# Splitting the modulation's first weights into two fp32r parts in a fused attention, mLSTM and expert block

## The chip, the cores and the metric

One core of one Trainium2 chip runs the whole program. The metric is the device time of one execution in microseconds (us). Five engines work side by side: TensorE (PE; its weight loads are listed as PEld), VectorE (DVE), ScalarE (ACT), GpSimd (POOL) and SyncE (SP), which here issues the DMAs.

## The reference, cut to what matters

One transformer block of depth 1 on 2048 tokens of width 1024, with 256 context tokens: modulation, an input projection, window attention and a two-way mLSTM beside each other, an output projection and an expert-choice FFN. The change is in the first two lines, of which `sh1` and `sc1` are needed before anything else can start:

```python
mod_x = silu(c)     @ w_mod + b_mod      # (1, 1024) @ (1024, 6144)
mod_c = silu(c_ctx) @ w_mod + b_mod
sh1, sc1, g1, sh2, sc2, g2 = split(mod_x, 6)          # the same split of mod_c
hx = rmsnorm(x, norm1_w) * (1 + sc1) + sh1            # 2048 tokens
hc = rmsnorm(ctx, norm1_w) * (1 + csc1) + csh1        # 256 context tokens
... = split(h @ w_in)                                 # 1024 x 2832, for hx and hc
```

## The kernel before, in words

The program has three phases: `phase_in` (modulation, projections, rope, convolution, window attention), `phase_mix` (mLSTM, output projection, router) and `phase_moe`. The change is in `phase_in`.

`phase_in` is written as coroutines (`Flow`). Each yields what it needs next: a token for a buffer (`tok[...]`), an event, or an engine with an estimated cost (`A(n)` ACT, `V(n)` DVE, `G(n)` POOL, `Q(n)` SP, or "P" with a number). A planner plays the engines through with these estimates and a priority for each coroutine (`PRI`, low number first), and emits the instructions in that order. So each engine has one fixed list and runs it strictly in order; a changed estimate or priority moves instructions far away from the edit. `BUFS` says how many buffers each name has.

- `mod_first` (L553) computes the two vectors' first 2048 columns of the modulation (shift and scale of the first norm). `sc8` holds silu(c) and silu(c_ctx): for each of the 8 blocks of 128 rows (k) and each of the 4 blocks of 512 columns (j) there are 8 stationary columns, of which two, at 2j and 2j+1, are not zero. So 32 matmuls (L593) in fp32 add up in one tile `rows` of 8x512. The weights come as `wm0` to `wm7`, 1 MB each, in `loads`. Then ACT copies `rows` out (L597), four small transposes (L603) turn it, and three DVE instructions (L608, L614) make `sh1` and `sc1`. In fp32 each of these matmuls is two records of the profile.
- `load_x` (L486) loads units of 256 tokens. `XW_AT` says behind which `wm` tile the first two units' loads (`xe`) and the first projection weights stand in SP's list. `norm_x` squares on ACT (L517), then scales on DVE (L522).
- `make_hx` (L628) transposes a unit (L689), applies scale and shift (`xv` or `hxv`, L653 and L658) and splits the result into `hx_hi` (rounded to fp32r) and `hx_lo` (the rest). `("x", 0)` is the first unit.
- `weights` (L702) loads the projection weights in pieces `w_raw` of 4 row blocks by 128 or 136 columns (three buffers), and `split_w` (L730) splits each into `w_hi` on ACT (L735) and `w_lo` on DVE (L741).
- `main` issues the projection as chains of 24 matmuls (L758, L776): hi by hi, lo by hi, hi by lo. The first group, "kv", goes unit by unit: x0, x1, then the context. Behind each kv chain stand rope and norm of the keys (`hxr`, `hr`, L947 to L966; products on POOL, L959 and L961), whose transposes (L1056 to L1058) stand in PE's list between later chains.

```python
rows = self.buf(self.ps, "o", [8, 512])
...
nc.tensor.matmul(rows, lhsT=sc8[:, k, j, :], rhs=ws[k][:, j * 512:(j + 1) * 512], ...)   # L593
```

## Time and profile before

| | |
|---|---|
| median of 3 runs | 2040.84 us (2037.56 to 2042.3) |
| the profiled execution | 2042.06 us |
| its span | 2040.3 us, so 1.8 us lie around it |
| TensorE busy | 91% of the span |
| VectorE, ScalarE, GpSimd busy | 78%, 63%, 41% |
| mean granted TensorE clock | 0.959 of full |

How to read it: times in rows are from the span's start. A busy TensorE is not a TensorE at its peak, since the ends of its matmuls are modelled and a later one starts while an earlier one drains; what one matmul costs in a run of them is the run's length by their number. A stall is worth what the chain of waits says it is worth in that stage, not the share of idle time over the whole span. The granted clock is 1.00 or 0.50 of full (2.4 or 1.2 GHz).

### The profile page before, as it was taken

To read this page: it belongs to the slowest core of one execution; us is meant where nothing else is said; L and a number is where in the kernel's file an instruction comes from. 1 tells how busy PE (TensorE), PEld (TensorE's weight loads), DVE (VectorE), ACT (ScalarE), POOL (GpSimd) and SP (SyncE) were. 2 spreads that over 40 slices of the span, in tenths; PEclk is the share of its full clock that TensorE was granted. 3 is DMA by queue.
4 is the path that set the end of the run, shared out by engine and by line. 5 is a ranking of instruction groups with operands and counts; after the bars stand their busy time and mean duration, and the time that the engine had idled before them with its cause. 6 is when DMAs were issued, how large, how long until landed. Compare 5 with 4: busy or idle time off the path is not lost.

```text
span 2040.3 us, 37000 instructions
## 1 busy us (share of the span) xinstructions
PE 1863.0 (91%) x12921; PEld 1665.6 (82%) x12921; DVE 1595.5 (78%) x3486; ACT 1280.7 (63%) x3144; POOL 839.1 (41%) x820
## 2 busy tenths in 40 slices
PE   7799999999999999996989989994589999999997
PEld 2698998899889989985767767783589999999996
DVE  3799779998998699868999677756667878787772
ACT  4477777787787777775665578865344545454542
POOL 0324234333543243316777665510334535353432
PEclk9899999999999999996999989996699999999999
DMA  8343264345342333227777867646467878888772
GB/s 281 98 145 102 73 189 123 109 149 160 99 120 79 95 84 97 79 82 205 270 255 260 286 224 242 225 145 222 133 203 210 261 226 253 240 235 254 223 233 42
DMA packets 293499, 357.82 MB, mean 175 GB/s; under 512 B 27288, under 2 KB 225592, under 8 KB 292416
## 3 DMA queue, kind: packets, MB, share of 16 engines
q1 hardware_dynamic: 283072, 320.32, 49.9%
q0 software_dynamic: 9376, 34.08, 7.2%
q8 instruction: 102, 1.67, 0.3%
q10 hardware_dynamic: 864, 1.05, 0.1%
q14 instruction: 85, 0.70, 0.1%
HBM read 270.73 MB, written 84.54 MB: 174 GB/s over the span
## 4 chain that ended last, share of the span: by engine, by line
PE 56%; DVE 24%; ACT 8%; DMA 6%; issue 5%; SPq 1%; POOL 0%; POOLq 0%; DVEq 0%; ACTq 0%
PE gu L2684 17%; PE mm L758 9%; PE yp L2736 8%; PE po L2004 5%; DVE w_lo L741 3%; PE t L303 2%; DMA w_raw<-in_w_in 2%; PE s L258 2%; PE o L593 1%; PE t L2628 1%; PE h L1912 1%; PE o L332 1%; PE o L331 1%; PE mm L776 1%; DVE s L280 1%
## 5 line engine op out<-in xcount | busy, mean ns | idle before, releaser
L2529 ACT ACTIVATE ew_hi<-ew_raw 128x1024 fp32r<-128x1024 f32 x184 | 193.6, 1056 | 163.6 <-PE yp L2736 91.5
L2457 DVE TENSOR_TENSOR ew_lo<-ew_raw,ew_hi 128x1024 fp32r<-128x1024 f32 x152 | 215.6, 1428 | 42.0 <-ACT ew_hi L2529 21.4
L291 POOL TENSOR_SCALAR P<-P,am 128x640 f32<-128x640 f32 (+1 forms) x128 | 113.1, 885 | 257.7 <-DVE am L289 145.4
L741 DVE TENSOR_TENSOR w_lo<-w_raw,w_hi 128x256 fp32r<-128x256 f32 (+1 forms) x352 | 157.3, 471 | 30.2 <-ACT w_hi L735 28.1
L2756 POOL DMA_INDIRECT out_x<-y,idx x32 | 57.1, 1786 | 260.7 <-DVE y L2750 175.0
L2684 PE MATMUL gu<-xg_hi,ew_hi 128*128 128x256 f32 x1024 | 148.6, 283 | 0.6 <-DVE xg_hi L2656 0.6
L758 PE MATMUL mm<-w_hi,hx_hi 128*128 128x256 f32 (+1 forms) x944 | 142.5, 288 | 5.2 <-ACT hxr L933 2.2
L735 ACT ACTIVATE w_hi<-w_raw 128x256 fp32r<-128x256 f32 (+1 forms) x352 | 135.2, 410 | 18.9 <-DMA w_raw<-in_w_in 18.1
L758 PE MATMUL mm<-w_hi,hx_lo 128*128 128x256 f32 (+1 forms) x944 | 141.9, 288 | 0.0
L2684 PE MATMUL gu<-xg_lo,ew_hi 128*128 128x256 f32 x1024 | 141.7, 280 | 0.0
L758 PE MATMUL mm<-w_lo,hx_hi 128*128 128x256 f32 (+1 forms) x944 | 141.5, 286 | 0.0
L2684 PE MATMUL gu<-xg_hi,ew_lo 128*128 128x256 f32 x1024 | 141.2, 280 | 0.0
L758 PEld LDWEIGHTS mm<-w_hi,hx_hi 128*128 128x128 f32 x944 | 124.8, 190 | 9.4 <-issue 2.7
L2684 PEld LDWEIGHTS gu<-xg_hi,ew_hi 128*128 128x128 f32 x1024 | 131.2, 189 | 1.0 <-DVE xg_hi L2656 0.9
L2684 PEld LDWEIGHTS gu<-xg_lo,ew_hi 128*128 128x128 f32 x1024 | 129.2, 189 | 0.0
L2684 PEld LDWEIGHTS gu<-xg_hi,ew_lo 128*128 128x128 f32 x1024 | 128.8, 189 | 0.0
L758 PEld LDWEIGHTS mm<-w_hi,hx_lo 128*128 128x128 f32 x944 | 125.0, 191 | 3.3 <-issue 2.6
L758 PEld LDWEIGHTS mm<-w_lo,hx_hi 128*128 128x128 f32 x944 | 124.6, 189 | 1.8 <-issue 0.9
L314 DVE TENSOR_TENSOR pl<-t,ph 128x512 fp32r<-128x512 f32 x156 | 105.8, 684 | 24.4 <-ACT ph L312 23.1
L282 ACT ACTIVATE P<-s,am 128x640 f32<-128x640 f32 (+1 forms) x128 | 99.8, 780 | 31.1 <-DVE am L280 25.7
L2750 DVE SCALAR_TENSOR_TENSOR y<-yp,gv,g2b 128x512 f32<-128x512 f32 x64 | 48.1, 751 | 90.2 <-PE yp L2736 90.2
L280 DVE CUSTOM_DVE_ANT_0 s<-s,mrow,nsink 128x640 f32<-128x640 f32 (+1 forms) x120 | 105.3, 877 | 13.1 <-PE s L262 7.5
(482 smaller groups left out, 5616.4 us busy)
## 6 DMA issues: line engine op xcount, KB each, us to landing
w_raw<-in_w_in SPq DMA_DIRECT2D x176, 256.0 KB
ew_raw<-in_w_gate SPq DMA_DIRECT2D x32, 1024.0 KB
ew_raw<-in_w_up SPq DMA_DIRECT2D x32, 1024.0 KB
ew_raw<-in_w_down SPq DMA_DIRECT2D x32, 1024.0 KB
xt<-in_w_mod SPq DMA_DIRECT2D x64, 256.0 KB
out_x<-xl SPq DMA_DIRECT2D x32, 512.0 KB
s_vs<-vsl SPq DMA_DIRECT2D x16, 516.0 KB
vsl<-s_vs SPq DMA_DIRECT2D x16, 516.0 KB
```

The source lines that it names most:

```text
L280: nc.vector.tensor_tensor_reduce(x, x, mask, 1.0, k.nsink[:, h:h + 1], op0=OP.add, op1=OP.min, accum_out=m[:, 0:1])
L282: nc.scalar.activation(P[:, :n], sc, AF.Exp, bias=m[:, 0:1], scale=-1.0, accum_out=m[:, 1:2])
L291: nc.gpsimd.tensor_scalar(P[:, :n], P[:, :n], m[:, 4:5], 0.0, op0=OP.mult, op1=OP.add)
L314: nc.vector.tensor_sub(lo, pt, f(hi))
L735: nc.scalar.activation(hi, raw[:, k:k + 2, :n], AF.Copy)
L741: nc.vector.tensor_sub(lo, raw[:, k:k + 2, :n], f(hi))
L758: self.nc.tensor.matmul(ps[:, :2 * n].rearrange("p (a b) -> p a b", a=2), lhsT=hx[:, k, t * 128:(t + 1) * 128], rhs=w[:, sl:sl + 2, k, :n] ...
L2004: self.nc.tensor.matmul(po, lhsT=m[:, k, :], rhs=self.wo[k0 + k][wi][:, sl], start=(j == 0), stop=(j == 11))
L2457: (self.nc.vector if eng == "D" else self.nc.gpsimd).tensor_sub(out, x, y)
L2529: nc.scalar.activation(hi[:, sl], raw[:, sl], AF.Copy)
L2684: nc.tensor.matmul(po[:, ft, :], lhsT=w[:, k, ft * 128:(ft + 1) * 128], rhs=x[:, k, :], start=(j == 0), stop=(j == 23))
L2736: nc.tensor.matmul(po[hf], lhsT=hs[i][h][:, ft, t * 128:(t + 1) * 128], rhs=wd[i][w][:, ft, hf * 512:(hf + 1) * 512], start=(j[hf] == 0), ...
```

## The change

The modulation's weights are split like the projection's: ACT rounds each 128x512 piece to fp32r (`mh`), and DVE takes the rest (`ml`), or POOL for the last piece of each of the first seven row blocks. silu is split as well (`sch` and the rest), and its two parts stand in 16 stationary columns instead of 8, hi at 2j and lo at 8+2j. Each piece then takes two fp32r matmuls against the same 16 columns, so that all four products add up in a tile of 16x512; two pieces of the last row block (`plain`) stay fp32. A ring of three buffers holds `mh` and `ml`. The four transposes become matmuls with `both` (two identities below each other), which add the two halves. The second unit's loads stand behind the first four pieces of projection weights (`w_first`) instead of before them, and the first unit's scaling and splitting (`hx0`) goes before everything else.

```diff
-XW_AT = (2, 6, 4, 7)
+XW_AT = (2, 7, 7, 7)
-PRI = dict(loadx=1, mod1=0, ..., hx0=1, ...)
+PRI = dict(loadx=1, mod1=0, ..., hx0=-1, ...)
-BUFS = dict(t=2, ...)
+BUFS = dict(mh=3, t=2, ...)
@@ load_x
                 if n < 2:
                     yield self.wm_ev[XW_AT[n]]
+                if n == 1:
+                    yield self.w_first
@@ mod_first
-        sc8 = p.tile([128, KT, 4, 8], F32, name="sc8")
-        nc.gpsimd.memset(sc8, 0.0)
+        s16, s16r = (p.tile([128, KT, 4, 16], dt, name=n) for n, dt in (("s16", F32), ("s16r", F32R)))
+        nc.gpsimd.memset(s16, 0.0)
+        sch = p.tile([128, KT, 2], F32R, name="sch")
+        both = p.tile([16, 8], F32, name="both")
...
-        for j in range(4):
-            yield V(16)
-            nc.vector.tensor_mul(sc8[:, :, j, 2 * j:2 * j + 2], self.c2, e)
-            fl.follow()
         yield V(16)
         nc.vector.tensor_mul(sc, self.c2, e)
+        yield V(16)
+        nc.vector.tensor_copy(sch, sc)
+        yield V(64)
+        nc.vector.tensor_copy(at(0), wide(f(sch)))
+        yield V(64)
+        nc.vector.tensor_sub(at(8), wide(sc), wide(f(sch)))
+        yield V2(512)
+        nc.vector.tensor_copy(s16r, s16)
+        yield V(8)
+        nc.vector.tensor_add(both, self.ident[0:16, 0:8], self.ident[0:16, 8:16])
...
+        plain = lambda k, j: k == KT - 1 and j < 2
...
-                if k == 0:
+                if k in (0, KT - 1):
...
+        def low(k, j, hi, lo, w):
+            if j == 3 and k < KT - 1:
+                yield G(512)
+                nc.gpsimd.tensor_sub(lo, w, f(hi))
+            else:
+                yield V(512)
+                nc.vector.tensor_sub(lo, w, f(hi))
...
+        def splits():
+            for k in range(KT):
+                for j in range(4):
+                    if plain(k, j):
+                        continue
+                    yield part[k][j]
+                    yield tok["mh"]
+                    hi, lo = (p.tile([128, 512], F32R, name=n, bufs=BUFS["mh"]) for n in ("mh", "ml"))
+                    w = ws[k][:, j * 512:(j + 1) * 512]
+                    yield A(512)
+                    nc.scalar.activation(hi, w, AF.Copy)
+                    fl.spawn(low(k, j, hi, lo, w), PRI["mod1"])
...
-                yield "P", 0.86
-                nc.tensor.matmul(rows, lhsT=sc8[:, k, j, :], rhs=ws[k][:, j * 512:(j + 1) * 512], ...)
+                if plain(k, j):
+                    yield part[k][j]
+                    yield "P", 0.86
+                    nc.tensor.matmul(rows, lhsT=s16[:, k, j, :], rhs=ws[k][:, j * 512:(j + 1) * 512], ...)
+                    continue
+                yield done[k][j]
+                yield "P", 0.46
+                for i, w in enumerate(pieces[k, j]):
+                    nc.tensor.matmul(rows, lhsT=s16r[:, k, j, :], rhs=w, ...)
+                fl.give(tok["mh"])
...
-            nc.tensor.transpose(pm[:, c, :], row8[:, c * 128:(c + 1) * 128], self.ident[:8, :8])
+            nc.tensor.matmul(pm[:, c, :], lhsT=row16[:, c * 128:(c + 1) * 128], rhs=both, start=True, stop=True)
@@ make_hx
-            fl.spawn(split(k2, pt, tag), PRI["hx0" if u == ("x", 0) else "hxsp"])
+            fl.spawn(split(k2, pt, tag), PRI["hx0"] + 0.1 * k2 if u == ("x", 0) else PRI["hxsp"])
@@ weights
+                    if n == 1:
+                        fl.fire(self.w_first)
```

SP's list between the loads of the first and of the second unit. The number in a name tells tiles apart; `xe` of before is the second unit here, `w_raw` are the projection weights. Before:

```order
L581 DMA wm_189<-in_w_mod 128x2048
L502 DMA xe_188<-in_x 128x1024
L502 DMA xe_199<-in_x 128x1024
L721 DMA w_raw<-in_w_in 128x4x128
L724 DMA w_raw<-in_w_in 128x4x8
```

With the change:

```order
L589 DMA wm_277<-in_w_mod 128x512 x4
L763 DMA w_raw<-in_w_in 128x4x128
L766 DMA w_raw<-in_w_in 128x4x8
L763 DMA w_raw<-in_w_in 128x4x128
L766 DMA w_raw<-in_w_in 128x4x8
L763 DMA w_raw<-in_w_in 128x4x128
L766 DMA w_raw<-in_w_in 128x4x8
L763 DMA w_raw<-in_w_in 128x4x128
L766 DMA w_raw<-in_w_in 128x4x8
L504 DMA xe_405<-in_x 128x1024
L504 DMA xe_413<-in_x 128x1024
```

The second unit has moved behind the fourth piece of weights, and that piece takes the first one's buffer.

ACT's list from the copy of the modulation's sums (`row`) to the first unit's `hx_hi`. Before, where the second unit's squares (L517 of `xe_188` and `xe_199`) stand ahead of the first of these rows:

```order
L597 ACTIVATE row_234<-o 8x512
L735 ACTIVATE w_hi<-w_raw 128x272 x2
L658 ACTIVATE xv_213<-t,sh_84,sc_83 128x256
L658 ACTIVATE xv_257<-tr,sh_84,sc_83 128x256
L735 ACTIVATE w_hi<-w_raw 128x272
L658 ACTIVATE xv_213<-t,sh_84,sc_83 128x256
L658 ACTIVATE xv_257<-tr,sh_84,sc_83 128x256
L735 ACTIVATE w_hi<-w_raw 128x272
L735 ACTIVATE w_hi<-w_raw 128x2x128
L663 ACTIVATE hx_hi_96<-xv_213 128x512
L735 ACTIVATE w_hi<-w_raw 128x2x128
L663 ACTIVATE hx_hi_96<-xv_257 128x512
```

With the change:

```order
L700 ACTIVATE xv_284<-t,sh_84,sc_83 128x256
L700 ACTIVATE xv_314<-tr,sh_84,sc_83 128x256
L700 ACTIVATE xv_284<-t,sh_84,sc_83 128x256
L700 ACTIVATE xv_314<-tr,sh_84,sc_83 128x256
L705 ACTIVATE hx_hi_96<-xv_284 128x512
L705 ACTIVATE hx_hi_96<-xv_314 128x512
L779 ACTIVATE w_hi<-w_raw 128x272
L519 ACTIVATE hxv,xss<-xe_405 128x1024
L519 ACTIVATE hxv,xss<-xe_413 128x1024
L779 ACTIVATE w_hi<-w_raw 128x2x128
L779 ACTIVATE w_hi<-w_raw 128x272
```

No weights stand between the first unit's scaling and its splitting any more; the second unit's squares stand behind both, and the eighth half piece of "kv" weights (the last row, 128x272) behind the squares.

PE's list at the context's kv chains (L758 before, L802 with the change; `hx_hi_386` and `hx_hi_588` are the context; the 128x128 rows of `hxr` are the ropes' transposes, one group of three for each 128 tokens). Before:

```order
L758 MATMUL mm<-w_hi,hx_hi_386 128x272 x4
L1056 MATMUL tr<-cst,hxr_428 128x128
L1057 MATMUL tr<-cst,gate 8x128
L1058 MATMUL tr<-cst,gate 8x128
L689 MATMUL tr<-cst,xt 128x128 x4
L1056 MATMUL tr<-cst,hxr_461 128x128
L1057 MATMUL tr<-cst,gate 8x128
L1058 MATMUL tr<-cst,gate 8x128
L758 MATMUL mm<-w_hi,hx_hi_386 128x272 x4
```

With the change:

```order
L1100 MATMUL tr<-cst,hxr_715 128x128
L1101 MATMUL tr<-cst,gate 8x128
L1102 MATMUL tr<-cst,gate 8x128
L802 MATMUL mm<-w_hi,hx_hi_588 128x272 x4
L1100 MATMUL tr<-cst,hxr_769 128x128
L1101 MATMUL tr<-cst,gate 8x128
L1102 MATMUL tr<-cst,gate 8x128
L731 MATMUL tr<-cst,xt 128x128 x8
L802 MATMUL mm<-w_hi,hx_hi_588 128x272 x4
```

All four rope groups (`hxr_715` and `hxr_769` are the third and fourth) now stand ahead of the context's second four matmuls; before, the third and fourth stood behind them.

## Rows read from the trace of the kernel before

**Rows 1.** Four stretches of the span: its bounds and length in us, busy us (and records) of each engine, then the granted clock, the share of the DMA engines and GB/s.

```profile
0.00:44.00 44.00, 33.53 (x92) 9.53 (x93) 11.63 (x46) 14.33 (x36) 0.65 (x6) 0.98 0.83 292
44.00:100.00 56.00, 43.59 (x301) 39.17 (x300) 41.58 (x130) 30.15 (x96) 14.78 (x22) 0.87 0.36 108
100.00:900.00 800.00, 768.62 (x5925) 723.88 (x5924) 699.51 (x1855) 607.86 (x1627) 286.82 (x408) 1.00 0.39 111
```

**Rows 2.** TensorE in order of time from the start: start us, length us, what, how many records, and in brackets the idle time before with what ended it.

```profile
7.79 25.88 PE L593 MATMUL o<-wm,sc 128*8 128x512 f32 x56 [7.79 <-DVE sc L561]
...
34.19 3.60 PE L593 MATMUL o<-wm,sc 128*8 128x512 f32 x8
...
39.18 0.41 PE L603 MATMUL mm<-cst,row 8*128 8x8 f32 x4
...
44.74 1.67 PE L758 MATMUL mm<-w_hi,hx_hi 128*128 128x272 f32 x8
...
52.01 1.17 PE L758 MATMUL mm<-w_lo,hx_hi 128*128 128x272 f32 x8
55.12 1.83 PE L758 MATMUL mm<-w_hi,hx_hi 128*128 128x272 f32 x8 [1.93 <-ACT hxr L933]
...
67.02 0.30 PE L1056 MATMUL tr<-cst,hxr 128*128 128x128 f32 x1 [0.52 <-issue]
...
73.67 1.09 PE L689 MATMUL tr<-cst,xt 128*128 128x128 f32 x4 [5.92 <-DVE gatet L1078]
75.97 0.45 PE L1056 MATMUL tr<-cst,hxr 128*128 128x128 f32 x1 [1.22 <-ACT hxv L658]
...
77.09 1.28 PE L758 MATMUL mm<-w_hi,hx_hi 128*128 128x272 f32 x4
```

**Rows 3.** DMA issues on SP and the first squares on ACT, in the same form.

```profile
17.70 0.38 SPq L721 DMA_DIRECT2D w_raw<-in_w_in  x1
...
35.32 0.37 SPq L721 DMA_DIRECT2D w_raw<-in_w_in  x1
...
17.71 1.06 ACT L517 ACTIVATE hxv<-xe 128x1024 bf16<-128x1024 f32 x1 [10.26 <-DMA xe<-in_x]
```

**Rows 4.** Windows of the modulation's stage, columns as in rows 1.

```profile
16.00:20.00 4.00, 4.00 (x11) 0.81 (x10) 0.00 (x0) 2.26 (x4) 0.00 (x0) 1.00 1.03 424
24.00:28.00 4.00, 4.00 (x11) 0.88 (x10) 0.00 (x0) 0.00 (x0) 0.00 (x0) 1.00 1.00 416
```

**Rows 5.** The nearest durations. First DVE at the preparation and at the first unit's scaling (first and last record), then DVE's and POOL's subtraction of 128x512 and ACT's rounding of 128x512, then a run of fp32r matmuls of 512 columns from the chain of waits (start us, length us).

```profile
7.56 0.43 DVE L561 TENSOR_TENSOR sc<-cols,sce 128x16 f32<-128x16 f32 x4 [0.36 <-ACT sce L551]
...
20.35 0.16 DVE L534 SCALAR_TENSOR_TENSOR rs_t<-xrs 128x1 f32<-128x1 f32 x1 [12.27 <-ACT xrs L532]
...
21.95 0.75 DVE L522 TENSOR_SCALAR xe<-xe,xrs 128x1024 f32<-128x1024 f32 x1
...
43.17 0.75 DVE L666 CAST hx_hi<-xv 128x512 fp32r<-128x512 f32 x2
...
47.04 1.29 DVE L670 TENSOR_TENSOR hx_lo<-xv,hx_hi 128x512 fp32r<-128x512 f32 x2
...
76.41 1.27 POOL L673 TENSOR_TENSOR hx_lo<-hxv,hx_hi 128x512 fp32r<-128x512 f32 x1 [2.20 <-DVE hx_hi L666]
...
43.18 0.63 ACT L663 ACTIVATE hx_hi<-xv 128x512 fp32r<-128x512 f32 x1
...
1528.50 10.90 PE yp L2736 x48
```

**Rows 6.** DVE and POOL at the same time, two places of the timeline.

```profile
251.56 2.19 DVE L741 TENSOR_TENSOR w_lo<-w_raw,w_hi 128x256 fp32r<-128x256 f32 x3
...
251.79 1.33 POOL L673 TENSOR_TENSOR hx_lo<-hxv,hx_hi 128x512 fp32r<-128x512 f32 x1 [2.43 <-PE mm L758]
...
1503.19 1.22 DVE L2457 TENSOR_TENSOR ew_lo<-ew_raw,ew_hi 128x1024 fp32r<-128x1024 f32 x1
...
1508.80 4.48 DVE L2457 TENSOR_TENSOR ew_lo<-ew_raw,ew_hi 128x1024 fp32r<-128x1024 f32 x1 [2.67 <-issue]
...
1508.56 1.29 POOL L2457 TENSOR_TENSOR xg_lo<-xv,xg_hi 128x512 fp32r<-128x512 f32 x1
1509.80 2.40 POOL L2457 TENSOR_TENSOR ew_lo<-ew_raw,ew_hi 128x1024 fp32r<-128x1024 f32 x1
```

**Rows 7.** Windows with TensorE partly idle, or just after idle time, columns as in rows 1.

```profile
8.00:10.00 2.00, 2.00 (x3) 0.27 (x2) 0.08 (x1) 0.00 (x0) 0.00 (x0) 1.00 1.05 436
12.00:14.00 2.00, 2.00 (x6) 0.45 (x5) 0.00 (x0) 0.00 (x0) 0.00 (x0) 1.00 1.00 422
42.00:44.00 2.00, 1.73 (x8) 1.73 (x9) 2.00 (x6) 1.81 (x5) 0.00 (x0) 0.50 0.92 250
62.00:66.00 4.00, 2.78 (x23) 2.32 (x21) 3.58 (x12) 2.92 (x10) 2.25 (x3) 1.00 0.00 0
1451.00:1457.00 6.00, 4.14 (x18) 3.37 (x19) 2.42 (x7) 3.07 (x7) 2.34 (x3) 0.50 0.04 3
```

**Rows 8.** What follows the modulation on ACT and DVE, in order of time: the copy of its sums, the first unit's first scaling, and the last product of the fourth rope.

```profile
37.83 0.59 ACT L597 ACTIVATE row<-o 8x512 f32<-8x512 f32 x1 [2.57 <-PE o L593]
...
40.42 0.57 ACT L658 ACTIVATE xv<-t,sh,sc 128x256 f32<-128x256 f32 x1 [1.37 <-DVE sc L614]
...
74.39 0.22 DVE L966 TENSOR_TENSOR hxr<-hxr,ropeu 128x64 f32<-128x64 f32 x1
```

More of the change, by code (lines that the diff above doesn't have):

```diff
@@ L456, in phase_in @@
             self.mod_ev, self.opened, self.main_done, self.rest_ev, self.turned = (Event() for _ in range(5))
-            self.att_ev, self.gt_ev = Event(), Event()
+            self.att_ev, self.gt_ev, self.w_first = Event(), Event(), Event()
             self.reach = {(b, g): Event() for b in range(4) for g in GROUPS}
@@ L581, in loads @@
                     nc.sync.dma_start(ws[k], a["w_mod"][k * 128:(k + 1) * 128, 0:2048])
+                    for ev in part[k]:
+                        fl.fire(ev)
                 fl.fire(self.wm_ev[k])
                 fl.issued()
+        def low(k, j, hi, lo, w):
[5 more added lines that the diff above has]
+                nc.vector.tensor_sub(lo, w, f(hi))
+            pieces[k, j] = hi, lo
+            fl.fire(done[k][j])
@@ L585, in mod_first @@
         fl.spawn(loads(), PRI["ml"])
+        fl.spawn(splits(), PRI["mod1"])
         for k in range(KT):
-            if k:
-                yield self.wm_ev[k]
             for j in range(4):
-                if not k:
-                    yield part[j]
-                yield "P", 0.86
-                nc.tensor.matmul(rows, lhsT=sc8[:, k, j, :], rhs=ws[k][:, j * 512:(j + 1) * 512],
-                                 start=(k == 0 and j == 0), stop=(k == KT - 1 and j == 3))
-        row8 = p.tile([8, 512], F32, name="row8")
+                if plain(k, j):
+                    yield part[k][j]
+                    yield "P", 0.86
+                    nc.tensor.matmul(rows, lhsT=s16[:, k, j, :], rhs=ws[k][:, j * 512:(j + 1) * 512], start=False, stop=False)
+                    continue
+                yield done[k][j]
+                yield "P", 0.46
+                for i, w in enumerate(pieces[k, j]):
+                    nc.tensor.matmul(rows, lhsT=s16r[:, k, j, :], rhs=w, start=(k + j + i == 0), stop=(k + j + i == KT + 3))
+                fl.give(tok["mh"])
@@ L596, in mod_first @@
+        row16 = p.tile([16, 512], F32, name="row16")
         yield A(512)
-        nc.scalar.activation(row8, rows, AF.Copy)
+        nc.scalar.activation(row16, rows, AF.Copy)
         fl.give(tok["o"])
@@ L609, in mod_first @@
                                  b.to_broadcast([128, 2, 2, 4]))
-            if j:
-                fl.follow()
+            fl.follow()
         fl.give(tok["mm"])
```

15 lines of the change are left out of this document (9 added, 6 removed).

## The prediction

> **What bounds the kernel now.** I read the chain of waits first, then the windows by stage, then the timelines of the first 100 us. From 100 to 900 us TensorE is busy 768.6 of 800 us at clock 1.00 [rows 1]: there a microsecond saved ahead of it is a microsecond saved at the end, and nothing that leaves TensorE's own work alone can bring much. The first 44 us have only 33.5 busy us of TensorE and the next 56 only 43.6 [rows 1]; the change works in these. The modulation's matmuls run without a pause from 7.79 to 37.79 us, with one group of transposes between them [rows 2]: TensorE is the bound there, not the DMA, which brings 416 to 424 GB/s throughout [rows 4]. The first projection chain starts at 44.74, the first unit's two chains end at 53.2, the second unit's first chain starts at 55.12, and from 67.4 to 77.1 TensorE has little but rope transposes to do; only at 77.09 does its continuous work begin [rows 2]. I call 37.79 the end of the modulation and 77.09 the point from which a shift is kept.
>
> **Term 1, the modulation's stage.** Removed: 64 fp32 records, 25.88/56 = 0.462 us each [rows 2], so 29.6 us of TensorE. Added: 60 fp32r matmuls at 10.90/48 = 0.227 us [rows 5] and 4 fp32 records, together 15.5 us. TensorE's need is halved, and the question is what becomes the bound.
> - DVE's preparation: six small instructions instead of five, of 0.2 us or less but for a cast of 512 columns (0.4); four of the five took 0.43 us [rows 5]. From 7.56 us I take 1.4 us, so the first subtraction can start at 9.0.
> - DVE subtracts 23 pieces (three in each of seven row blocks, two in the last). Two such instructions in a row took 1.29 and one takes 0.68, so 0.61 each [rows 5]: 14.0 us.
> - POOL subtracts 7 pieces of 1.27 us [rows 5]: 8.9 us. Do the two engines do it side by side? Rows of this case say no. At 251.56 three subtractions of 0.42 took 2.19 us, because one stood still while POOL's ran to 253.12; at 1508.80 one that takes 1.22 alone took 4.48, through two of POOL's, 1.29 and 2.40 [rows 6]. So one row block costs 3 x 0.61 + 1.27 = 3.1 us, above the 2.5 us in which 1.05 MB come at 420 GB/s [rows 4], and the sum is 22.9 us.
> - The first unit's scaling stays between the row blocks on DVE, 20.35 to 22.70 [rows 5]: 2.35 us. ACT's two squares, 1.06 us each [rows 3], now stand between roundings of 0.6 us [rows 5] for which DVE waits, and the second row block's data come a little late for DVE: 1.6 us together.
> - Tail: behind the last of POOL's pieces TensorE runs the two pieces left in fp32, 4 x 0.462 = 1.85, and two split ones, 0.9; 1.2 us of DVE's work in the sum runs beside that, so 1.6 more.
>
> 9.0 + 22.9 + 2.35 + 1.6 + 1.6 = 37.5, against 37.79: **-0.3 us**. Bounds: if POOL's subtractions fell into gaps of DVE and the DMA were the limit, 9.44 MB at 0.42 MB per us with 1.4 MB there at 8 us are in at 28, the last piece needs its rounding, subtraction and matmuls, and the stage ends near 31: -7. If TensorE ran at half clock, 60 x 0.454 + 4 x 0.92 = 30.9 from 9.0, and four groups of transposes make it 41.5: +3.7. I take the value by the exclusion, since two places of this trace show it.
>
> **Term 2, from there to the end of the first unit's kv chains.** The sums' copy starts at 37.83 and the first scaling at 40.42, 2.6 us later [rows 8], with transposes and weight splits between; with the change neither stands there, so 0.59 + 0.41 + three small DVE instructions give 1.6: -1.0. The first unit is then scaled and split without weights between, so `hx_hi` is there 4.7 us after the end of the modulation. But the eighth half piece of weights stands on ACT behind the second unit's two squares, which cost ACT nothing on the path before. They wait for a load that is issued only when the fourth piece of weights has its buffer: that issue stood at 35.32 [rows 3] and stays near 36.5, because the buffer is freed by DVE behind its last subtraction. I have the squares start at +5 us and the eighth half at +7.6, so the first chain's last two matmuls come at +8, against 46.41 - 37.79 = +8.6 before; then the second unit's normalization (two DVE instructions of 0.75 [rows 5]) holds up its transposes in the middle of the second chain. The two effects leave **-0.5 us**, bounds -2 (all of the shorter path stays) and +3 (second unit late by as much as its squares and scaling take, 2.1 + 1.5, less 0.6).
>
> **Term 3, to the continuous work.** The four rope groups now all stand ahead of the context's second four matmuls; before, two did. The fourth rope's last product was done at 74.39 [rows 8], before TensorE reached 77.09, so the two moved groups add no wait of their own unless the second unit comes later, and what TensorE has left afterwards is shorter by two groups of up to 1.1 us each (75.97 to 77.09 [rows 2]). **-1.0 us**, bounds -4 and +4 (one context tile's transposes, scaling and POOL subtractions earlier or later; POOL took 1.27 for each of four).
>
> **Term 4, the rest of the first phase.** The planner moves instructions everywhere up to 900 us and none behind. TensorE's idle time there is 31.4 us of 800 [rows 1]; I take 0 and keep +-3 for another order of the same work.
>
> **Sum.** -0.3 - 0.5 - 1.0 = -1.8 us, so the profiled execution's 2042.06 becomes 2040.3. The median of the runs shown, 2040.84, lies 1.2 us below the profiled execution, so I give **2039.0 us**. A measurement of this kernel can tell about 0.2% from no change, 4.1 us: faster is below 2036.8, slower above 2044.9.
>
> **Rivals.**
> - *Faster: the DMA becomes the bound.* POOL has only one piece in four and the ring of three lets ACT run ahead, so POOL's piece could start where DVE would wait anyway. Against it stand the two places of rows 6, for it that the second of them had two POOL instructions in a row and this stage never has. Term 1 is then -5 to -7, and with the others about -7.5: 2033. Chance 0.34.
> - *Slower: TensorE's clock.* Today TensorE starts slowly (3 records in 2 us from 8 us on, 6 at 12 us [rows 7]) and then works without a pause. With the change it has 8 x 0.227 = 1.8 us of work for each 3.1 us. From 62 to 66 us it was busy 2.78 of 4 us and kept 1.00, but from 1451 to 1457 it was busy 4.14 of 6 and stayed at 0.50, and behind the idle time before 42 us it was at 0.50 too [rows 7]. The price: +3.7 in term 1, and the first unit's chains entered at half clock, where eight 272-column matmuls took 1.83 us instead of 1.17 [rows 2], for some four groups of eight: +2.6; the other terms' gains are then -1.0. It decides if half clock holds for more than half of the stage, since below that the subtractions are the slower part. 2040.84 + 5.3 = 2046. Chance 0.16. The Trainium skill, "TensorE: Matmul & The Clock Gate", section "A second HAM failure mode: psum-queue depth-cycling", tells of a kernel whose TensorE paused briefly and often between groups of matmuls and swung between the two clocks. By that rule this stage would swing too and cost about half of the first price, 1.9 us; the trace has stretches for it and against it.
> - *Slower: the second unit comes late.* Its loads wait in SP's list behind a buffer that DVE frees only behind the modulation; if that moves squares, transposes and ropes back together, terms 2 and 3 are at their upper bounds, +7 - 0.3: 2047. For it: before, its loads stood ahead of all weights. Against it: ACT is busy with the first unit until they can be there. Chance 0.08.
>
> **How the numbers follow.** The forecast, no change that can be measured, has 0.42, and its own range, from half of each term's bounds, is 2036 to 2043. The first rival gives faster, 0.34, the other two slower, 0.24. The range reaches into the rivals' times: 2031.5 to 2046.5 leaves out the first rival's far end (all of -7 and a better order) and the ends of the two slow ones, 0.2 together.
>
> **What would show it.** Right: `mh` and `ml` in about 3.1 us for a row block, subtractions of DVE that take 1.9 us where one of POOL's begins in front of them, the copy of the sums near 37.5, and continuous work on TensorE from about 75 us. For the first rival: row blocks at 2.5 us and the copy near 31 to 33. For the second: clock 0.50 in most of 10 to 37 us and fp32r matmuls of 0.45. For the third: TensorE waiting for `xe` transposes beyond 54 us. The forecast is wrong if the copy comes by 33 or after 40, or if TensorE's idle time from 100 to 900 us changes by more than 3 us.

## The result: slower by 1.2%, and the profile after

The changed kernel took **2065.14 us** (median of 4 runs, 2063.97 to 2067.02) against 2041.57 of the kernel before on the same chip; ratio **1.0119, 95% interval 1.0102 to 1.0137**, some 24 us. The two profiled spans, 2040.3 and 2062.2 us, differ by 21.9. The forecast was 2039.0 with a range from 2031.5 to 2046.5: the change went the other way, and the time lies outside the range.

Windows of the changed kernel by stage, columns as in [rows 1], and then one window in the idle stretch:

```profile
0.00:44.00 44.00, 26.41 (x89) 9.18 (x89) 28.53 (x60) 27.17 (x56) 10.48 (x13) 0.91 0.79 273
44.00:100.00 56.00, 35.04 (x179) 29.18 (x180) 30.33 (x101) 26.43 (x82) 10.47 (x16) 0.64 0.20 58
100.00:900.00 800.00, 767.80 (x5896) 721.16 (x5895) 698.89 (x1849) 598.98 (x1605) 282.34 (x407) 1.00 0.40 115
...
74.00:94.00 20.00, 8.50 (x30) 4.52 (x30) 8.58 (x26) 6.55 (x22) 5.32 (x7) 0.50 0.06 16
```

Against [rows 1] the first 44 us have 7 busy us of TensorE less, as the split should bring. The next 56 have 179 records where 301 stood, at clock 0.64 and not 0.87. From 100 to 900 us the busy time hardly differs (767.8, 768.6). This points to the stretch between the modulation's end and 100 us; the milestones below show it. From 74 to 94 us TensorE is busy 8.5 of 20 us, and all of it at the lower level of 1.2 GHz.

TensorE of the changed kernel in order of time, the same places as [rows 2] (L731 is L689 of before, L802 is L758, L1100 to L1102 are L1056 to L1058, L1122 is L1078):

```profile
36.37 1.89 PE L631 MATMUL o<-wm,s 128*16 128x512 f32 x4
...
39.96 1.05 PE L646 MATMUL mm<-both,row 16*128 16x8 f32 x8 [0.68 <-ACT row L640]
43.97 1.73 PE L802 MATMUL mm<-w_hi,hx_hi 128*128 128x272 f32 x6 [2.96 <-ACT hx_hi L705]
47.50 0.82 PE L802 MATMUL mm<-w_hi,hx_hi 128*128 128x272 f32 x2 [1.80 <-ACT w_hi L779]
48.12 2.02 PE L802 MATMUL mm<-w_hi,hx_lo 128*128 128x272 f32 x8
...
59.90 1.27 PE L802 MATMUL mm<-w_hi,hx_hi 128*128 128x272 f32 x4 [2.15 <-DVE hx_hi L708]
63.88 0.82 PE L802 MATMUL mm<-w_hi,hx_hi 128*128 128x272 f32 x2 [2.70 <-DVE hx_hi L708]
...
72.78 0.63 PE L731 MATMUL tr<-cst,xt 128*128 128x128 f32 x4 [1.19 <-DVE gatet L1122]
74.76 0.45 PE L1100 MATMUL tr<-cst,hxr 128*128 128x128 f32 x1 [1.35 <-ACT hr L534]
75.00 0.42 PE L1101 MATMUL tr<-cst,gate 128*8 128x128 f32 x1
75.36 0.59 PE L1102 MATMUL tr<-cst,gate 128*8 128x128 f32 x2
79.46 1.08 PE L731 MATMUL tr<-cst,xt 128*128 128x128 f32 x4 [3.52 <-DVE gatet L1122]
81.71 0.45 PE L1100 MATMUL tr<-cst,hxr 128*128 128x128 f32 x1 [1.16 <-ACT hxv L700]
...
85.87 0.45 PE L1100 MATMUL tr<-cst,hxr 128*128 128x128 f32 x1 [1.77 <-DVE gatet L1122]
...
90.02 1.08 PE L731 MATMUL tr<-cst,xt 128*128 128x128 f32 x4 [2.97 <-DVE gatet L1122]
92.28 1.12 PE L731 MATMUL tr<-cst,xt 128*128 128x128 f32 x4 [1.17 <-ACT hxv L700]
...
95.03 0.82 PE L802 MATMUL mm<-w_hi,hx_hi 128*128 128x272 f32 x2 [1.18 <-DVE hx_hi L708]
```

Read the brackets from 72.78 to 92.28: each group of transposes waits for the copies of the group ahead of it, since all of them go through the one buffer `tr`. (The bracket at 74.76 names `hr`; ACT's last copy out of `tr`, `hxv`, ended at 74.67, 0.1 us before.) The continuous work, that is matmuls of the projection one behind the other, starts at 95.03, where it started at 77.09 [rows 2].

The kernel before had the first three of the context's four transposes ahead of the first rope (67.02 [rows 2]), between chains:

```profile
60.77 0.60 PE L689 MATMUL tr<-cst,xt 128*128 128x128 f32 x4
...
62.73 0.62 PE L689 MATMUL tr<-cst,xt 128*128 128x128 f32 x4
...
64.68 0.66 PE L689 MATMUL tr<-cst,xt 128*128 128x128 f32 x4 [0.82 <-ACT hxv L658]
```

Inside one of these turn-rounds, the rope that began at 81.71, on all engines (first and last of each kind): four ACT copies, four DVE subtractions and the gate's copy, then the next group may begin.

```profile
82.30 0.60 PE L1102 MATMUL tr<-cst,gate 128*8 128x128 f32 x2
...
82.93 0.27 ACT L1112 ACTIVATE kt<-tr 64x128 fp32r<-64x128 f32 x1 [1.32 <-PE tr L1102]
...
83.78 0.27 ACT L1114 ACTIVATE kt<-tr 64x128 fp32r<-64x128 f32 x1
84.08 0.28 DVE L1118 TENSOR_TENSOR kt<-tr,kt 64x128 fp32r<-64x128 f32 x1 [2.02 <-ACT kt L1114]
...
85.31 0.41 DVE L1122 COPY gatet<-tr 8x256 f32<-8x256 f32 x1
```

From the transpose at 81.71 to the next group's at 85.87 a rope holds `tr` for 4.16 us, of which TensorE works 1.2. A context transpose holds it for 2.25 (79.46 to 81.71). From 72.78 to 95.03 four context transposes hold it for 9.2 us and three ropes for 13.0: that is the whole 22.25 us (the last of them up to the matmul that needs its result). Before the change only one turn-round of a rope was waited for, 5.92 us [rows 2].

The milestones, in us from the span's start: the copy of the modulation's sums 37.83 before and 39.32 after, the first projection matmul 44.74 and 43.97, the end of the first unit's kv chains 53.2 and 57.5, of the second unit's 63.9 and 71.6, the continuous work 77.09 and 95.03, the first projection matmul of L776 (L820 after) 96.7 and 115.1, the last hi-by-hi one of L758 (L802) 906.1 and 927.2, the first of the experts 1456.6 and 1477.9. Eighteen of the 21 us are lost by 95 us.

What the 21 us consist of, from 40 us to that last hi-by-hi matmul (before, after):

```profile
40.00:906.00 866.00, 819.94 (x6278) 770.56 (x6278) 747.93 (x2003) 645.57 (x1742) 302.99 (x432) 0.99 0.39 111
```

```profile
40.00:927.00 887.00, 830.88 (x6285) 776.69 (x6286) 750.33 (x2010) 650.07 (x1751) 299.71 (x432) 0.97 0.38 109
```

TensorE's idle time grew from 46.1 to 56.1 us (length less busy), and its busy time by 10.9 us, at clock 0.97 in place of 0.99. So half of the loss is waiting and half is longer busy time. One us of the latter is the modulation's own transposes (39.96), which lay ahead of 40 us before. A part comes with the lower level of the clock. Its stretches up to 100 us, first of the kernel before, then of the changed one:

```profile
41.90:45.30 3.40, 3.03 (x14) 3.03 (x15) 3.40 (x10) 2.55 (x7) 0.00 (x0) 0.50 0.94 302
55.60:59.00 3.40, 3.40 (x17) 3.40 (x16) 2.73 (x11) 0.50 (x2) 0.00 (x0) 0.50 0.00 0
69.20:79.50 10.30, 4.61 (x18) 3.42 (x19) 5.75 (x23) 2.65 (x9) 3.81 (x7) 0.50 0.24 77
```

```profile
43.30:53.50 10.20, 7.72 (x32) 7.41 (x33) 8.49 (x25) 7.14 (x22) 0.00 (x0) 0.50 0.69 195
60.30:67.20 6.90, 4.20 (x18) 3.82 (x18) 6.06 (x24) 3.11 (x10) 1.41 (x3) 0.51 0.00 0
74.00:97.90 23.90, 11.37 (x43) 7.39 (x43) 9.01 (x27) 7.07 (x22) 6.63 (x8) 0.50 0.12 35
```

With one more such stretch of the kernel before behind 100 us (345.7 to 349.1) and two of the changed one (347.0 to 350.5, 418.7 to 422.1), TensorE was busy at the lower level for 14.5 us before and 30.2 after. Eight matmuls take 1.17 us at the upper level [rows 2] and 2.02 at the lower, so by an estimate these 15.7 us more cost 6.6 us. The remaining 3 us of longer busy time were not traced to a cause.

### The profile page after: what moved, and what is told of

It is laid out like the page before. It is cut to its first block, busy times and chain, and to the rows that moved or that the text cites. A ratio compares the mean times of both kernels' runs of the same rounds, so it can differ in the third digit from the quotient of the medians.

```text
span 2062.2 us, 37117 instructions
## 1 busy us (share of the span) xinstructions
PE 1867.1 (91%) x12925; PEld 1672.0 (81%) x12925; DVE 1616.3 (78%) x3510; ACT 1297.6 (63%) x3174; POOL 844.4 (41%) x827
## 4 chain that ended last, share of the span: by engine, by line
PE 55%; DVE 24%; ACT 8%; DMA 6%; issue 5%; POOL 1%; SPq 0%; POOLq 0%; DVEq 0%; ACTq 0%
PE gu L2728 17%; PE mm L802 9%; PE yp L2780 8%; PE po L2048 5%; DVE w_lo L785 3%; PE t L303 2%; DMA w_raw<-in_w_in 2%; PE s L258 2%; PE mm L820 2%; PE t L2672 1%; PE o L332 1%; PE o L331 1%; PE h L1956 1%; DMA wm<-in_w_mod 1%; DVE s L280 1%
## 5 line engine op out<-in xcount | busy, mean ns | idle before, releaser
L802 PE MATMUL mm<-w_hi,hx_hi 128*128 128x256 f32 (+1 forms) x944 | 146.1, 291 | 11.1 <-DVE hx_hi L708 6.0
L802 PE MATMUL mm<-w_lo,hx_hi 128*128 128x256 f32 (+1 forms) x944 | 141.9, 289 | 0.0
L802 PE MATMUL mm<-w_hi,hx_lo 128*128 128x256 f32 (+1 forms) x944 | 141.1, 289 | 0.0
L802 PEld LDWEIGHTS mm<-w_hi,hx_hi 128*128 128x128 f32 x944 | 126.9, 192 | 15.1 <-DVE hx_hi L708 7.0
L802 PEld LDWEIGHTS mm<-w_lo,hx_hi 128*128 128x128 f32 x944 | 126.1, 192 | 2.6 <-issue 1.7
L802 PEld LDWEIGHTS mm<-w_hi,hx_lo 128*128 128x128 f32 x944 | 125.7, 192 | 1.0 <-issue 0.4
```

Of the source, the lines that this page charges most:

```text
L802: self.nc.tensor.matmul(ps[:, :2 * n].rearrange("p (a b) -> p a b", a=2), lhsT=hx[:, k, t * 128:(t + 1) * 128], rhs=w[:, sl:sl + 2, k, :n] ...
```

## The experiments

Three theories were tested. Theory 1: the planner's new order puts the four ropes between the context's transposes, and the turn-round of `tr` is the loss. Theory 2: the split modulation itself comes late (half clock, late second unit). Theory 3: SP's list, blocked by the gate's stores, holds up loads.

The results together. "Ropes" is how many ropes stand ahead of the fourth context transpose on TensorE; then the start of the first matmul of L776 and of the last hi-by-hi one of L758 (whatever its line in that kernel), TensorE's idle and busy time from 40 us to there, and the time against the kernel before on the same chip. All columns but the last are of the one profiled execution, which for ctx_t and hx0_old took 5.7 and 4.8 us more than the median of the kernel, and for before_new_order 4.8 less.

| kernel | ropes | first L776 | last L758 | idle / busy | ratio (95%) |
|---|---|---|---|---|---|
| before | 1 | 96.7 | 906.1 | 46.1 / 819.9 | 1 |
| changed | 4 | 115.1 | 927.2 | 56.1 / 830.9 | 1.0119 (1.0102 to 1.0137) |
| split_only | 1 | 97.7 | 908.6 | 48.3 / 820.7 | 1.0005 (0.9995 to 1.0015) |
| order_only | 4 | 116.0 | 929.4 | 58.0 / 831.0 | 1.0110 (1.0084 to 1.0137) |
| ropes_last | 0 | 97.9 | 916.1 | 46.2 / 829.8 | 1.0053 (1.0036 to 1.0070) |
| ctx_t | 1 | 98.3 | 921.0 | 53.3 / 827.7 | 1.0075 (1.0058 to 1.0091) |
| hx0_old | 4 | 112.6 | 927.5 | 56.0 / 831.0 | 1.0116 (1.0099 to 1.0133) |
| xw_old | 2 | 100.5 | 911.5 | 48.1 / 822.9 | 1.0032 (1.0020 to 1.0045) |
| split_dve | 4 | 113.8 | 928.5 | 57.9 / 830.1 | 1.0117 (1.0099 to 1.0135) |
| before_ropes_last | 0 | 91.9 | 908.0 | 41.2 / 826.8 | 1.0008 (0.9998 to 1.0017) |
| before_new_order | 4 | 113.4 | 929.0 | 56.9 / 832.1 | 1.0137 (1.0118 to 1.0157) |
| after_old_order | 1 | 104.3 | 915.7 | 49.3 / 826.7 | 1.0034 (1.0022 to 1.0046) |
| dve_old_order | 1 | 100.0 | 910.0 | 47.6 / 822.4 | 1.0043 (1.0028 to 1.0058) |
| after_t | 4 | 111.3 | 927.7 | 56.5 / 831.5 | 1.0109 (1.0093 to 1.0125) |
| after_ropes_t | 4 | 107.9 | 925.7 | 54.9 / 831.1 | 1.0086 (1.0069 to 1.0103) |
| before_ropes_t | 1 | 92.3 | 905.7 | 44.1 / 821.9 | 0.9984 (0.9973 to 0.9995) |
| split_ropes_t | 1 | 92.0 | 905.1 | 42.3 / 822.7 | 0.9993 (0.9978 to 1.0008) |

**The two halves of the change.** split_only is the changed kernel with `XW_AT`, `w_first` and the priority `hx0` as before; order_only is the kernel before with those three as after.

```diff
 split_only
-XW_AT = (2, 7, 7, 7)
+XW_AT = (2, 6, 4, 7)
-                if n == 1:
-                    yield self.w_first
-hx0=-1 ... PRI["hx0"] + 0.1 * k2 if u == ("x", 0) else PRI["hxsp"]
+hx0=1 ... PRI["hx0" if u == ("x", 0) else "hxsp"]
```

> The split weights and the split vector alone, with the loads, the second unit's condition and the first unit's priority as before the change. Theory 1: the planner puts three context transposes ahead of the first rope, as before the change, so the loss goes: 2038 to 2046 us. Theory 2: the modulation is what is late, 2057 to 2066 us.

> The opposite half: the fp32 modulation of before, with the changed order of loads, the changed condition of the second unit and the changed priority. The planner puts all four ropes ahead of the context's second four matmuls here too. Theory 1: the loss is nearly whole, 2056 to 2066 us, with the continuous work starting at 90 to 96 us. Theory 2: 2037 to 2046 us, since the modulation is the one of before.

1.0005 and 1.0110, 2044.2 and 2064.1 us, both as theory 1 says. The split by itself moves the time by nothing that can be measured, the three lines of order bring nearly the whole loss. Theory 2 falls for the modulation; for the late second unit it is not decided yet, since `w_first` is among the three lines.

**Which line.** hx0_old gives back the priority alone, xw_old the loads alone.

```diff
 hx0_old
-hx0=-1 ... PRI["hx0"] + 0.1 * k2 if u == ("x", 0) else PRI["hxsp"]
+hx0=1 ... PRI["hx0" if u == ("x", 0) else "hxsp"]
 xw_old
-XW_AT = (2, 7, 7, 7)
+XW_AT = (2, 6, 4, 7)
-                if n == 1:
-                    yield self.w_first
```

> The changed kernel with the priority of the first unit's preparation as before; the changed order of the loads stays. In the planned order two ropes stand among x1's chains and two, not three, between the context's transposes. Theory 1 (each rope between two context transposes costs its turn-round of tr, about 4 us): the continuous work starts 4 to 8 us earlier than after the change, at 87 to 91 us, and the time is 2056 to 2061 us. Theory 2 (the split modulation, or the late loads, delay the stage whatever the order): 2063 to 2067 us.

> The changed kernel with the order of the loads as before (x1 after the seventh row block of the modulation, the first two weight blocks after the fifth, no condition on the second unit); the split and the changed priority of the first unit stay. In the planned order two context transposes stand ahead of the first rope and three ropes among the rest, where before the change there are three and two. Theory 1: one turn-round more than before the change, 4 to 6 us: the continuous work starts at 81 to 84 us, the time is 2045 to 2050 us. If the order of the loads alone is the cause: 2040 to 2045 us; if the priority alone is: 2060 to 2066 us.

xw_old took 2048.9 us, in the range of theory 1, with the start at 80.8. hx0_old does not fit it: its start came at 92.3 and the time, 2066.0, is in theory 2's range. Counting the ropes between the transposes and multiplying by 4 us is too simple, since a rope ahead of all of them holds `tr` as well: its second rope, among the second unit's chains, held `tr` from 69.24 to the end of its gate's copy at 74.73, and TensorE sat idle for 3.24 us before the first context transpose at 74.88. Between late loads and the order these two runs do not decide.

**The order alone.** These kernels do. split_dve differs from split_only by one condition, and its planned order turns by itself. before_new_order and after_old_order force the order of the ropes and the context transposes by events (`ct_ev` fires behind each context transpose, `rp_ev` behind each rope's matmuls), each into the other kernel.

```diff
 split_dve (on split_only)
-            if j == 3 and k < KT - 1:
+            if j == 9:
                 yield G(512)
 before_new_order, after_old_order, dve_old_order (WAIT differs)
         yield ev
+        if not ctx and n < 4:
+            for i in WAIT_ROPE[n]:
+                yield self.ct_ev[i]
         yield tok["tr"]
...
         for k2, tag in enumerate(tags):
+            if u == ("c", 0):
+                for i in WAIT_CTX[k2]:
+                    yield self.rp_ev[i]
             yield tok[tag]
 new: WAIT_ROPE = [], [0], [1], [1]; WAIT_CTX = [0], [1], [3], [3]
 old: WAIT_ROPE = [2], [3], [3], [3]; WAIT_CTX = [], [], [], [0]
```

> The split alone (loads and priority as before), with all subtractions of the split on DVE and none on POOL. Without the mutual exclusion of DVE and POOL the modulation's sums should end some 2 to 3 us earlier, at 36 to 37 us in place of 39. But the planner's order turns: all four ropes again stand ahead of the context's last transposes, though loads and priority are those of before. Theory 1: the order decides, and the kernel is as slow as the changed one less those 2 to 3 us, 2058 to 2064 us, with the continuous work from 90 to 94 us. If the order of the loads or the priority act by themselves, not through the place of the ropes: 2039 to 2044 us.

> The kernel before (fp32 modulation, loads and priority as before), with events that force the first four ropes and the context's four transposes into the order of the changed kernel; behind the sums the planned order of TensorE is then that of the changed kernel but for the first unit's chains. Theory 1 (the place of the ropes is the whole loss): continuous work from 92 to 95 us, time 2059 to 2065 us. If modulation, loads or the late second unit carry a good part of it: 2045 to 2055 us.

> The opposite: the changed kernel with events that force the ropes and the context's transposes into the order of before (three context transposes, one rope, the fourth transpose, the second rope, the others within the continuous matmuls). The order of TensorE from there to the end of the projection is then that of before. Theory 1: the loss goes but for the 4 to 8 us by which x0's and x1's chains end later, and these are partly covered by the wait of 5.9 us for the first rope: 2041 to 2048 us. If the changed loads and the second unit cost by themselves what x1's chains show (7.75 us later): 2048 to 2052 us. If the order is not the cause: 2060 to 2066 us.

split_dve took 2066.3 us, 2 us above its range. Its sums were copied at 36.77, 2.2 us ahead of split_only's 38.98, and still it is as slow as the changed kernel. before_new_order, with the fp32 modulation and the old loads, took 2067.3, also 2 us above its range: the order alone brings the whole loss, 1.0137 against the changed kernel's 1.0119. Its second unit's chains end at 65.2, 1.3 us later than in the kernel before, and its continuous work starts at 93.29, 16.2 us later. Its TensorE stands in the same chain of waits (same form as above):

```profile
71.33 1.09 PE L693 MATMUL tr<-cst,xt 128*128 128x128 f32 x4 [4.02 <-DVE gatet L1089]
73.57 0.45 PE L1065 MATMUL tr<-cst,hxr 128*128 128x128 f32 x1 [1.16 <-ACT hxv L659]
...
77.71 1.09 PE L693 MATMUL tr<-cst,xt 128*128 128x128 f32 x4 [2.95 <-DVE gatet L1089]
79.95 0.45 PE L1065 MATMUL tr<-cst,hxr 128*128 128x128 f32 x1 [1.16 <-ACT hxv L659]
...
93.29 0.82 PE L764 MATMUL mm<-w_hi,hx_hi 128*128 128x272 f32 x2 [1.18 <-DVE hx_hi L667]
```

after_old_order gave back 17 us, to 2048.6 (1.0034), at the lower edge of its second range, not in theory 1's. The 7 us left are there by its first L776 matmul, which comes 7.6 us later than in the kernel before. So with the changed kernel's modulation, loads and priority the order is worth 17 us, and with those of before it is worth all 24: the two shares do not add up. What the late loads cost by themselves no run shows, since after_old_order keeps the new modulation and priority too. Theory 3 has nothing for it: from 57 to 96 us of the changed kernel no wait on TensorE, ACT or DVE ends at a DMA.

**The old order with the faster sums.**

> The split alone, with all its subtractions on DVE, loads and priority as before, and the order of before forced. With the order turned this kernel took 2066.3 us, though its sums ended 2.2 us earlier than with the subtractions shared with POOL. Theory 1: the order of before gives back all of it and the earlier sums remain: 2038 to 2043 us, the continuous work from 75 to 77 us, no more than 3 us ahead of the kernel before and perhaps none.

Missed: 2048.5 us, start at 80.3. The order gives back 18 us of split_dve's loss, but the earlier sums do not turn into time. The first unit's chains began without the second unit's transposes ahead of them, and eight of their matmuls took 2.0 us (clock 0.78 from 40 to 100 us, split_only 0.86). Its second unit's chains end at 69.1, 5.2 us later than in the kernel before, although its loads and priority are those of before: so the remainder of after_old_order need not be the late loads either. Its profiled execution took 2045.2 us, 3.3 below its median, so that the profile does not show all of it; this stays open.

**The ropes behind the context.** One wait more, in the changed kernel and in the one before: a rope asks for `tr` only when the last piece of the context's `hx_hi` is there.

```diff
         yield ev
+        if not ctx and n < 4:
+            yield self.hh_ev["c", 0][3]
         yield tok["tr"]
```

> The changed kernel, with one wait more: a rope group asks for the buffer tr only after the context's last transposes have been issued. Theory 1 (the four rope groups, each holding tr some 4 us through PE, ACT and DVE, stand between the context's transposes and push the continuous work from 77 to 95 us): the context's transposes come one after another again, the continuous work starts 14 to 18 us earlier, at 77 to 81 us, and the time is 2047 to 2051 us. Theory 2 (the split modulation itself is late: half clock, second unit late, and the ropes only stand in an idle that is there anyway): at most 4 us come back, 2061 to 2065 us. Theory 3 (SP's queue is blocked by the gate's stores and the loads behind them are late): no more than 4 us come back either, and the wait in front of the continuous work ends at a DMA.

> The kernel before, with the wait that puts the ropes behind the context's transposes. The changed kernel with this wait began its continuous work at 77 us, where the kernel before begins it, and was still 11.7 us slower than that: some 9 us were lost between 98 and 916 us. If that loss comes with the wait itself (another planned order of the attention behind it), this kernel is slower than before too, although its continuous work begins earlier, at about 70 to 72 us in place of 77: 2043 to 2051 us. If it comes with the changed modulation or loads, this kernel gains: 2034 to 2039 us.

Both start as theory 1 says, at 77.2 and 70.5 us, but the time is 2054.4, above the range, and 2044.0, not told from no change. The table tells where it went: in before_ropes_last TensorE's idle time fell by 4.9 us and its busy time rose by 6.9, in ropes_last the idle time is the kernel before's and the busy time 9.9 longer. Behind the first L776 matmul both have four stretches at the lower level of the clock (before_ropes_last from 178.5, 335.5, 547.2 and 594.9 us on), where the kernel before has one (from 345.7). They hold 13.7 and 13.6 us of TensorE's busy time against 3.4. By the 1.17 and 2.02 us above this costs an estimated 4.3 us, of the 6.7 that before_ropes_last and the 8.8 that ropes_last lost between the table's two matmuls. Why the clock falls more often in these orders is not shown; the wait may well move more than the four ropes, since the planner decides anew behind it.

**The buffer or the queue.** ctx_t gives the context's transposes the buffers `t`, in an order of the planner's own; after_t does so in the changed order, forced; after_ropes_t leaves them in `tr` and puts the first four ropes into `t`.

```diff
 ctx_t, after_t
-        tags = {("x", 0): ("t", "t", "tr", "mm"), ("x", 1): ("t", "t", "tr", "t")}.get(u, ("tr",) * 4)
+        tags = {("x", 0): ("t", "t", "tr", "mm"), ("x", 1): ("t", "t", "tr", "t"), ("c", 0): ("t",) * 4}.get(u, ("tr",) * 4)
 after_ropes_t, before_ropes_t, split_ropes_t
-        yield tok["tr"]
-        pt = self.buf(self.ps, "tr", [128, 3, 128])
+        tag = "tr" if ctx or n >= 4 else "t"
+        yield tok[tag]
+        pt = ...
```

> The changed kernel, with the context's transposes in the buffers named t in place of tr; the ropes stay where they are in the order. Theory 1: the transposes no longer wait for a rope's copies, and most of 14 to 18 us come back, 2047 to 2053 us. If it is the place of the ropes on TensorE's queue rather than the shared buffer, little comes back: the ropes still wait for each other in tr, each 4 us, ahead of the continuous work, 2055 to 2062 us. Theories 2 and 3: 2061 to 2066 us.

> The changed kernel in the changed order (forced by events; only the first context transpose moves ahead by one chain), with the context's transposes in the buffers named t, so that only the ropes still pass tr among themselves. If the sharing of the one buffer is what makes the order dear: the transposes no longer wait 3.5 and 3.0 us for a rope's copies nor a rope 1.2 to 1.4 us for a transpose's, the continuous work starts at 84 to 88 us in place of 95, and the time is 2052 to 2058 us. If the order costs through TensorE's queue alone, whatever the buffer: 93 to 96 us and 2062 to 2066 us.

> The changed kernel in the changed order (forced by events; the first context transpose one chain earlier), with the first four ropes in the two buffers named t in place of the one named tr. No rope then waits for a transpose's copies, no transpose for a rope's, and a rope for the one before the last. If the turn-round of the shared buffer is the cost: the waits of 3.5, 1.8 and 3.0 us for the gate's copy go, the continuous work starts at 78 to 84 us in place of 95, and the time is 2046 to 2055 us. If the cost is that TensorE's queue is in order and the ropes' inputs are late: waits for the DVE products of the ropes take their place, the start is at 88 to 95 us, and the time 2059 to 2066 us.

ctx_t took 2059.2 us, the time of its second case, but not by its mechanism: its ropes came to stand among the chains and its continuous work started at 77.3. It lost its time later (idle 53.3, busy 827.7), and so tells little of the buffer. after_t fell between its two cases at the start, at 90.4 us, and its time, 2063.7, is that of the second. after_ropes_t too started between its cases, at 86.4, 8.7 us earlier than the changed kernel, and its time, 2060.8, is that of the second. Its TensorE, between:

```profile
76.54 0.30 PE L1112 MATMUL t<-cst,hxr 128*128 128x128 f32 x1 [2.28 <-DVE hxr L1016]
...
79.80 0.45 PE L1112 MATMUL t<-cst,hxr 128*128 128x128 f32 x1 [2.54 <-DVE hxr L1016]
...
83.61 1.11 PE L735 MATMUL tr<-cst,xt 128*128 128x128 f32 x4 [1.58 <-ACT hxv L701]
86.36 0.82 PE L808 MATMUL mm<-w_hi,hx_hi 128*128 128x272 f32 x2 [1.18 <-DVE hx_hi L709]
```

Up to this start no wait for `gatet` is left; waits for the ropes' own products `hxr` have come in their place. So theory 1 as stated is a part of it. Of the 8.7 us, 2.0 stood already at the second unit's first chain (57.88, where the changed kernel has 59.90), so the shared buffer is worth some 6.7 of the 17.9 us at the start. Another part is that a rope whose product is late stands on TensorE's queue ahead of transposes that are ready (2.28 and 2.54 us here), and 4.3 us of the 17.9 had been lost before, by the end of the first unit's chains. Why most of the 8.7 us are gone by 926 us (last hi-by-hi L758 matmul 1.5 us earlier only) was not settled; the profiled execution took 3.0 us more than the median.

**A version that is faster.** The kernel before and split_only with the first four ropes in `t`, old order forced up to the second rope.

> The kernel before in its own order up to the second rope (forced), with the first four ropes in the buffers named t. If the wait of 5.9 us ahead of the fourth context transpose is the turn-round of tr, it goes and the continuous work starts 4 to 6 us earlier, at 71 to 73 us. By what the earlier start brought where the ropes were put last (5 us earlier at the start, nothing at the end), the time is 2038 to 2044 us; if the start carries through, 2036 to 2038 us.

> The split with loads and priority as before, in the order of before up to the second rope, with the first four ropes in the buffers named t. The same as for the kernel before, later by the 1.0 us by which the split's continuous work starts later: start at 72 to 74 us, time 2037 to 2045 us.

before_ropes_t started at 72.1 and took 2040.3 us, 0.9984 (0.9973 to 0.9995): faster by 3 us (1 to 5.5), within the first of its ranges, and the only kernel here that is faster than the one before by more than its interval. split_ropes_t started at 70.3, ahead of its range, and took 2040.5: 0.9993 (0.9978 to 1.0008), not told from no change. In both, 2.6 us of waiting for `hxr` are left of the 5.9 that were there for the gate's copy.

## Why the prediction was wrong

**Bound: right.** The first 100 us were the place, and 100 to 900 us stayed full. The terms are counted below as the prediction cut them: to the end of the modulation, to the end of the first unit's chains, to the continuous work. They came to +1.5, +2.8 and +13.6, together 17.9 us, where -0.3, -0.5 and -1.0 were said. One sum does not come out: half of each term's bounds, added up, reaches from 2032 to 2047 and not from 2036 to 2043.

**Term 1, the modulation: small, the sign wrong.** -0.3 was said, +1.5 came (39.32 against 37.83 [rows 8]), within the bounds. The exclusion of DVE and POOL showed as predicted. DVE and POOL of the changed kernel: three subtractions with none of POOL's ahead, and three where one of POOL's began 0.4 us before:

```profile
8.89 1.88 DVE L607 TENSOR_TENSOR ml<-wm,mh 128x512 fp32r<-128x512 f32 x3
...
32.23 2.61 DVE L607 TENSOR_TENSOR ml<-wm,mh 128x512 fp32r<-128x512 f32 x3 [0.35 <-ACT mh L621]
```

```profile
31.81 1.27 POOL L604 TENSOR_TENSOR ml<-wm,mh 128x512 fp32r<-128x512 f32 x1 [3.79 <-ACT mh L621]
```

The Trainium skill, "SBUF — State Buffer", section "🎯 Summary: rules for kernel authors", says that a DVE instruction with two SBUF inputs and a GpSimd one that reads SBUF do not run side by side, the later one waits; the 2.61 us against 1.88, and split_dve's sums 2.2 us earlier without POOL, agree. What I missed are DVE's waits for ACT's roundings `mh`: 1.58 us at 12.34, 1.14 at 27.51, 1.28 at 31.19 (1.6 us in all was allowed for such waits). The faster rival (a stage near 31 us) did not come.

**Term 2: 3.3 us too low, just within its bound of +3.** The first unit's chains ended 4.3 us later, 1.5 of which is term 1, so +2.8 came where -0.5 was said. The eighth half piece of weights came late as described (a wait of 1.80 us at 47.50, 8.2 us behind the modulation's end where +8 was said), but these chains then ran at half clock up to 53.5 us, where eight matmuls took 2.02.

**The late second unit, the third rival.** Its loads were issued at 39.17, where they had been issued at 13.93 and where about 36.5 was said; its squares began at 44.64 in place of 30.27, and its chains ended 7.75 us later. The rival was priced at 2047 with a chance of 0.08, and after_old_order, which has the late loads without the new order, took 2048.6. That is no proof of the rival's price: dve_old_order lost as much with the loads of before, and the ropes did not move back with the squares (the first stood at 67.19, where it had stood at 67.02). That a time near the rival's came out may be luck.

**Term 3: this step failed.** It said that "the two moved groups add no wait of their own unless the second unit comes later", and gave -1.0 with bounds of -4 and +4; +13.6 came. The condition does not save it, since before_new_order, whose second unit is 1.3 us late, starts its continuous work 16.2 us later all the same. The term asked when a rope's input is ready (74.39 [rows 8]) and how long TensorE works on it (1.1 us), and not how long the rope keeps the one buffer that the next group on the queue needs: 4.16 us, through ACT and DVE. The wait that shows this price was in my own rows, [5.92 <-DVE gatet L1078] at 73.67 [rows 2], and I read past it. The term also looked at two moved ropes only, and the order had changed at another place: three context transposes that had stood ahead of the first rope now stood behind it, so that six groups (three ropes, three transposes) passed `tr` one behind the other ahead of the last transpose. The clock, at 0.50 from 74.0 us on, was no part of the term either.

**Term 4: nearly right.** Idle time from 100 to 900 us is 32.2 us, against 31.4 [rows 1]; some 3 us of the loss lie behind 95 us, at the edge of the +-3. Neither of the two signs by which the forecast was to be wrong came (39.32 is not after 40, 0.8 us is not 3): they looked at both sides of the stretch in which the loss arose. The sign for its being right, continuous work from about 75 us, failed by 20 us.

**The clock, the second rival.** From 0 to 44 us it was 0.91, so not half for most of the modulation, and that price, +3.7, did not come. Its other price did in part: the first unit's chains ran at half clock. No term and no rival had the lower level from 74.0 to 97.9 us, behind the idle time. The Trainium skill, "TensorE: Matmul & The Clock Gate", section "A second HAM failure mode: psum-queue depth-cycling", which the prediction cites, tells of a clock that swings between its two levels. Here it swung once in the modulation (1.00 from 8 to 20 us, 0.50 from 24 to 28, 1.00 from 32 to 40) and stayed low through the stretch that cost the time.

## What to carry to other kernels

Where several small jobs share one PSUM buffer, a job's price on an in-order engine is how long it holds the buffer until the last copy, not its own time there: write down hold times before judging a new order. When a change alters a planner's inputs, compare the planned order at each shared buffer first; here one condition on the engine of a subtraction turned it and cost 22 us (split_only against split_dve), and forcing the order by events, the new one into the old kernel and the old one into the new, told the cause in two runs. Where waits overlap, the shares of two causes do not add up: the same order was worth 24 us in the old kernel and 17 in the changed one. And when TensorE has to wait, count the work that is then done at the lower clock too.

## What was not expected of the hardware

An earlier start was not kept in three kernels. before_ropes_last began its continuous work 6.6 us ahead of the kernel before and came to its last hi-by-hi L758 matmul 1.9 us behind it; ropes_last began with the kernel before and came there 10.0 us behind it; after_ropes_t began 8.7 us ahead of the changed kernel and came there 1.5 us ahead. In the first two TensorE was busy 6.9 and 9.9 us longer than in the kernel before, at a mean clock of 0.98 in place of 0.99. How many falls of the clock a planned order brings was not to be seen from its idle time: before_ropes_last has the least idle time of all, four falls of the clock behind its first L776 matmul against one, and is no faster.
